# Row of the norm, first activations of down, and two first tiles: four pieces of work placed elsewhere in a one-core encoder block

## The chip, the core and the metric

The kernel runs on one core of a Trainium2 chip. A core has five engines with queues of their own: PE (TensorE, matmuls; its weight loads are listed apart as PEld), DVE (VectorE), ACT (ScalarE), POOL (GpSimd) and SP (SyncE, which here only issues transfers). The metric is the time on the device of one execution, in microseconds (us). Three runs of the kernel before gave 1122.03 to 1122.51 us, with a median of 1122.2 us.

## What is computed

One layer of an encoder block on 256 tokens of width 2048, in float32. Two mixers (a state-space scan in both directions and a pooling mixer) read one projection and share an output projection; a gated channel mixer follows, and then a gated embedding:

```python
h = h + rmsnorm(mix, mix_norm_post[i])
hn = rmsnorm(h, ffn_norm_pre[i])
up = hn @ w_up                                    # 2048 -> 2 x 5632
gate, val = jnp.split(up, 2, axis=-1)
gate = dwconv_centred(gate, conv_w, conv_b)       # 3 taps along the tokens
ff = (jax.nn.gelu(gate, approximate=True) * val) @ w_down   # 5632 -> 2048
h = h + rmsnorm(ff, ffn_norm_post[i])
gate = jax.nn.sigmoid(rmsnorm(h, ple_norm_pre[i]) @ w_ple_gate[i])
h = h + rmsnorm(gate * (p[i] @ w_ple[i]), ple_norm_post[i])
```

The change touches the part from "hn" to the gate's product. The stages are called wo (the output projection), up, down (dn), the embedding (ple) and the gate (gt).

## The kernel before

**Split numbers.** Each float32 operand is split into a high half (a cast on ACT, line 153) and a low half (source minus high half, a subtraction on DVE, line 154); a product is then three matmuls: high by high, high by low, low by high. The function is `split` (line 142). Raw weights arrive in a ring of three buffers of 1 MB (`raw`, line 157), the halves of 1024 columns go to rings of five (`whi`, `wlo`). A split whose name stands in `ready` was made earlier; one in `spare` has its own place. Larger tiles are pages, of which there are 13 (line 74).

**Who sets the order.** A planner orders the instructions of each engine by the order of the program and by its own estimate of when each is ready; a data dependency becomes a semaphore. `tc.issue_after(i)` puts what is traced inside behind instruction i on i's engine. Inside `with in_order():` (line 199) ACT, DVE and SP run exactly in the order of the program; PE is not bound by it.

**Up** (lines 966 to 980) is such an ordered block. It has 176 pieces, each of 512 rows by 256 columns of the weight, in order of slab (512 columns), gate or value, and half (256 columns); four pieces make a sum, in two accumulators. Five pieces are split ahead; at piece n, after its matmuls are traced, a finished sum is taken out (n % 4 == 3), piece n + 5 is split (`next_part`), then the convolution of the last gate's sum (`gate_conv`, at n % 4 == 0) and its gelu (n % 4 == 1) follow, and then the jobs kept for that piece (`jobs_at`): fetching, adding and storing the block sums of later weights (line 253), and sums of hidden activations. The gate's sums (`gate_out`, line 935) are multiplied by the row `rfb`, the reciprocal norm of each token laid along the tokens (line 941). The norm's factor comes out of `row_rstd` (line 398) as one number per partition; `along_tokens` (line 408) turns it: for each half of the tokens DVE copies the number to 128 columns (line 414), PE multiplies that with the identity, and DVE copies the result back (line 416). Up calls it ahead of its ordered block (line 876), and the first stage does so for its own row (line 535).

**Down** (`sublayer`, line 819, called on line 1036) has two halves of 1024 output columns, each of 22 units of two rows of tiles (`token_major`, line 305). Fifteen units of a half use seven products instead of eight (`seven_products`, line 255), for which sums of weight blocks, made in up and kept in DRAM, and sums of activations are loaded; the plain units are 0, 1, 6, 10, 17, 20 and 21. A plain unit has 24 matmuls of 512 columns, the others 21. The activations of a unit are split in `get_hid` (lines 989 and 990) into one of two buffers hs; all of these splits stand behind the last instructions of up's ordered block on ACT and DVE. `at` gives jobs to run ahead of a unit, in the second half only: ahead of unit 11 the first tile of the gate is loaded to a page and split to two more, and after the last unit the first tile of the embedding's second half is loaded and split in the rings, and the saved rows of h come back.

**The boundary.** After down's last sum come the norm, the new rows of h (line 848), their transposes (dnxt, line 391) and the split panel (dnx, lines 190 and 191), while PE has the embedding's matmuls to do; then the gate's.

Of the kernel before, what the change touches and what calls it, by code (L numbers as in the profile page):

```python
# [11 lines left out]
F32 = mybir.dt.float32  # L12
F32R = mybir.dt.float32r
AF = mybir.ActivationFunctionType
ALU = mybir.AluOpType
ORDERED = (mybir.EngineType.Activation, mybir.EngineType.DVE, mybir.EngineType.SP)

P = 128
L = 256
# [5 lines left out]
NF = DFF // P  # L25
# [28 lines left out]
def build(nc, a, out):  # L54
# [6 lines left out]
    with tile.TileContext(nc) as tc, \  # L61
# [15 lines left out]
        def mid(name, dtype=F32):  # L77
            return gp.tile([P, 1024], dtype, tag="mid", bufs=3, name=name)
# [10 lines left out]
        def mm(o, lhsT, rhs, start, stop):  # L89
            last["pe"] = ins(nc.tensor.matmul(o, lhsT, rhs, start=start, stop=stop, skip_group_check=True))  # L90
# [317 lines left out]
        def along_tokens(name, r):  # L408

            rb = sp.tile([P, L], F32, tag="rb", bufs=1, name=name)  # L410
            ps = misc(f"{name}p")
            for t in range(2):
                w = mid(f"{name}w{t}")
                nc.vector.tensor_copy(w[:, :P], r[t][:, 0:1].to_broadcast([P, P]))
                mm(ps[:, t * P:(t + 1) * P], w[:, :P], ident, True, True)
            nc.vector.tensor_copy(rb, ps[:, :L])
            return rb

# [397 lines left out]
                return dict(self.got[k], a11=(h1[:, :P], l1[:, :P]), a12=(h2[:, :P], l2[:, :P]),  # L816
                            a22=(h2[:, P:], l2[:, P:]))

        def sublayer(name, w, ks, get, gain, h, vnext, panel=Panel, fast=((), ()), sums=None, at=(), row=None):

            mg = [page(f"{name}m{t}") for t in range(2)]
            sq = [[], []]
            for half in range(2):
# [2 lines left out]
                acc = [main(f"{name}a{half}{t}") for t in range(2)]  # L826
                if fast[half]:
                    alt += main(f"{name}s{half}") if half else []
                token_major(f"{name}{half}", w, half * 1024, ks, get, acc, 1, fast[half], alt, sums, at if half else ())
                for t in range(2):  # L830
                    for n in range(2):
                        q = tiny(f"{name}q{t}{half}{n}", 1)
# [40 lines left out]

        pl = [ple(0)]
        rf = row_rstd("rf", h)
        rfb = along_tokens("rfb", rf)
        h_kept = []
        for t in range(2):
            h_kept.append(dp.tile([P, D], F32, tag=f"h{t}", bufs=1, name=f"h_kept{t}"))
# [18 lines left out]
        def hid_part(k):  # L898
            return hid[k // 8][:, (k % 8) * L:(k % 8 + 2) * L]

        def hid_sums_of(k, s, o):
            return pair_sums(f"he{k}", s, o, *(hid_part(k)[:, i * P:(i + 1) * P] for i in range(4)))

# [14 lines left out]
        for u in dn_stored:  # L918

            jobs_at[16 * (u // 2) + 4 * (u % 2) + 13].extend(hid_sums_jobs(2 * u))  # L920

        blocks = [(s, v, i) for s in range(DFF // 512) for v in range(2) for i in range(2)]
        parts, slab = [], {}
# [11 lines left out]
        def gate_out(s, i, acc):  # L935
            if i == 0:
                slab[s] = mid(f"gr{s}"), mid(f"fc{s}"), mid(f"ft{s}")
            o = slab[s][0][:, i * 512:(i + 1) * 512]
            total(o, acc)
            v = o.rearrange("p (f t) -> p f t", f=2)  # L940
            nc.vector.tensor_tensor(v, v, rfb.unsqueeze(1).to_broadcast([P, 2, L]), op=ALU.mult)

        def gate_conv(s, i):

# [21 lines left out]
        with in_order():  # L966
            for _ in range(5):
                next_part()
            for n in range(NPIECES):
                s, v, i = blocks[n // 4]  # L970
                if n % 4 == 0:
                    acc = main(f"{'gv'[v]}a{s}{i}")
                feature_pairs(n % 4, parts[n], hf, acc)
                if n % 4 == 3:
                    (value_out if v else gate_out)(s, i, acc)
                next_part()
                if n >= 4 and n % 4 < 2 and blocks[n // 4 - 1][1] == 0:
                    (gelu if n % 4 else gate_conv)(blocks[n // 4 - 1][0], blocks[n // 4 - 1][2])
                for job in jobs_at[n]:
                    job()  # L980
        ends = [chain[e] for e in ORDERED[:2]]

        cur = {}

        def get_hid(k):
            if k % 2 == 0:
                t = lp.tile([P, 1024], F32R, tag="hs", bufs=2, name=f"hs{k}")
                with tc.issue_after(ends[0]), tc.issue_after(ends[1]):
                    nc.scalar.copy(t[:, :512], hid_part(k))  # L989
                    nc.vector.tensor_sub(t[:, 512:], hid_part(k), t[:, :512].bitcast(F32))  # L990
                cur["t"] = t
            o = (k % 2) * L
            return cur["t"][:, o:o + L], cur["t"][:, 512 + o:512 + o + L]

# [17 lines left out]
                d = hid_sums_of(k, sp.tile([P, 512], F32, tag="junk", bufs=1, name=f"hs{k}"), o)  # L1012
            return dict(d, a11=(h1[:, :P], l1[:, :P]), a12=(h2[:, :P], l2[:, :P]), a22=(h2[:, P:], l2[:, P:]))

        def ple_parts():

            r = raw("ple1r0", w_ple[1, 0])
            for j in range(2):
                ready[f"ple10_{j}"] = split(f"ple10_{j}", r[:, j * 1024:(j + 1) * 1024], 1024)

        def back():

            for t in range(2):
                h[t] = page(f"hb{t}")
                last["dma"] = load(h[t], h_kept[t])

        def first():

            r, hi, lo = page("gtf"), page("gtfh", F32R), page("gtfl", F32R)
            last["dma"] = load(r, w_gate[0, 0])  # L1030
            for j in range(2):
                c = slice(j * 1024, (j + 1) * 1024)
                spare[f"gt00_{j}"] = hi[:, c], lo[:, c]
                ready[f"gt00_{j}"] = split(f"gt00_{j}", r[:, c], 1024)

        hp = sublayer("dn", w_down, list(range(NF)), hid_get, gload("gffn", a["ffn_norm_post"][0]), h, V_PN,
                      fast=dn_fast, sums=hid_sums, at={11: first, NF // 2: lambda: (ple_parts(), back())}, row=rf)


        pl = [page("plb")]  # L1040
# [154 lines left out]
```

## Time and profile before

| | |
|---|---|
| median of three runs | 1122.2 us |
| profiled execution | 1122.17 us |
| its span, first to last instruction | 1120.3 us |
| PE busy | 1107.4 us (99%), 5957 matmuls |
| DVE busy | 942.4 us (84%) |
| ACT busy | 716.7 us (64%) |
| POOL busy | 65.3 us (6%) |
| transfers | 336.54 MB, 300 GB/s in the mean |
| granted clock of PE | 0.999 |

A row of the timeline has the start in us from the span's start, the duration, the engine, the line of the program, the operation, output<-inputs (buffer numbers left out), the shape and the count; in brackets stands how long the engine had been idle before and what ended that. Matmuls overlap, so one that lasts 0.39 us is followed by the next after 0.23 us, and a busy PE is not yet a PE at its pace; gaps are read from starts. A list of waits has the engine, its instruction, what it waited for, the time in total, the count and the longest. Stages by that clock: wo until about 286 us, up from 293 to 788 us, down from 790 to 1014 us, the gate from 1020 us.

### The profile page before, as it was taken

What the parts mean: (1) busy time and instruction counts of PE and PEld (TensorE: products, weight loads), DVE (VectorE), ACT (ScalarE), POOL (GpSimd) and SP (SyncE); (2) the same over time, 40 slices, a digit from 0 to 9 for tenths busy, and PEclk for the clock granted to TensorE, in tenths of its full rate; (3) what the DMA queues carried; (4) which work ended last, traced back from release to release, by engine and by line L of the source; (5) the groups of instructions that cost most, each with busy time, mean ns of one, the idle gap of its engine ahead of it and who ended that gap; (6) DMA issues with size and microseconds to landing.
All of it is one profiled execution on the core that took longest, in us unless ns stands there. A gap on an engine that the chain in (4) does not pass through costs nothing.

```text
span 1120.3 us, 15956 instructions
## 1 busy us (share of the span) xinstructions
PE 1107.4 (99%) x5957; PEld 952.8 (85%) x5957; DVE 942.4 (84%) x1300; ACT 716.7 (64%) x1039; POOL 65.3 (6%) x133
## 2 busy tenths in 40 slices
PE   9999999999999999999999999999999999999997
PEld 9999988888888888888888888888788888877876
DVE  6569897899878888888878888888799899989795
ACT  6847663555775564655655656656688778867573
POOL 0200000100100000000000000000000000001001
PEclk9999999999999999999999999999999999999999
DMA  9752446454599999999889898989898799996663
GB/s 363 310 208 96 171 159 270 151 188 178 230 366 389 361 353 367 360 343 352 359 322 373 326 383 345 356 346 374 322 408 313 242 348 405 413 362 238 228 232 107
DMA packets 53070, 336.54 MB, mean 300 GB/s; under 512 B 5888, under 2 KB 6784, under 8 KB 19072
## 3 DMA queue, kind: packets, MB, share of 16 engines
q1 hardware_dynamic: 43200, 284.03, 65.6%
q0 software_dynamic: 9360, 50.86, 12.4%
q8 instruction: 47, 0.77, 0.3%
q10 hardware_dynamic: 432, 0.62, 0.2%
q14 instruction: 31, 0.25, 0.1%
HBM read 290.92 MB, written 44.56 MB: 299 GB/s over the span
## 4 chain that ended last, share of the span: by engine, by line
PE 94%; DVE 2%; ACT 2%; issue 1%; POOL 0%; DMA 0%; SPq 0%; POOLq 0%; ACTq 0%
PE va L90 22%; PE ga L90 21%; PE dna L90 12%; PE woa L90 7%; PE xbc L90 6%; PE gt L90 5%; PE z L90 4%; PE dtu L90 4%; PE dns L90 4%; PE dn0s L90 2%; PE dn1s L90 2%; PE pw L90 1%; PE yd L90 1%; PE ple L90 1%; DMA dtur<-w_dtu 0%
## 5 line engine op out<-in xcount | busy, mean ns | idle before, releaser
L90 PE MATMUL ga<-wox,ug_0h 128*128 128x512 f32 x352 | 125.6, 395 | 0.0
L90 PE MATMUL ga<-wox,ug_1h 128*128 128x512 f32 x352 | 125.1, 394 | 0.0
L90 PE MATMUL va<-wox,uv_0h 128*128 128x512 f32 x352 | 124.8, 393 | 0.0
L90 PE MATMUL va<-wox,uv_1h 128*128 128x512 f32 x352 | 124.7, 393 | 0.0
L90 PE MATMUL ga<-wox,ug_1l 128*128 128x256 f32 x352 | 99.1, 282 | 0.0
L90 PE MATMUL ga<-wox,ug_0l 128*128 128x256 f32 x352 | 99.1, 282 | 0.0
L90 PE MATMUL va<-wox,uv_0l 128*128 128x256 f32 x352 | 99.1, 281 | 0.0
L90 PE MATMUL va<-wox,uv_1l 128*128 128x256 f32 x352 | 98.9, 281 | 0.0
L253 DVE TENSOR_TENSOR dnb<-dnb 128x512 f32<-128x512 f32 x120 | 82.8, 690 | 3.1
L90 PEld LDWEIGHTS va<-wox,uv_0h 128*128 128x128 f32 x352 | 66.1, 188 | 15.0
L90 PEld LDWEIGHTS ga<-wox,ug_0h 128*128 128x128 f32 x352 | 66.1, 188 | 14.9
L90 PEld LDWEIGHTS ga<-wox,ug_1h 128*128 128x128 f32 x352 | 66.1, 188 | 14.9
L90 PEld LDWEIGHTS va<-wox,uv_1h 128*128 128x128 f32 x352 | 66.1, 188 | 14.9
L90 PEld LDWEIGHTS ga<-wox,ug_0l 128*128 128x128 f32 x352 | 66.2, 188 | 0.1
L90 PEld LDWEIGHTS va<-wox,uv_1l 128*128 128x128 f32 x352 | 66.2, 188 | 0.1
L90 PEld LDWEIGHTS ga<-wox,ug_1l 128*128 128x128 f32 x352 | 66.2, 188 | 0.0
L90 PEld LDWEIGHTS va<-wox,uv_0l 128*128 128x128 f32 x352 | 66.2, 188 | 0.0
L989 ACT CAST hs<-hid 128x512 fp32r<-128x512 f32 x44 | 27.2, 621 | 24.5 <-PE dna L90 24.3
L990 DVE TENSOR_TENSOR hs<-hid,hs 128x512 fp32r<-128x512 f32 x44 | 30.1, 686 | 10.2 <-ACT hs L989 10.2
L90 PE MATMUL dna<-dn_0h,hs 128*128 128x512 f32 x112 | 35.4, 394 | 1.8 <-issue 1.5
L90 PE MATMUL dna<-dn_1h,hs 128*128 128x512 f32 x112 | 35.6, 393 | 0.0
L244 POOL DMA_DIRECT2D dns<-dnb x28 | 15.2, 543 | 321.6 <-DVE dnb L253 297.3
(2128 smaller groups left out, 3159.6 us busy)
## 6 DMA issues: line engine op xcount, KB each, us to landing
dnb<-w_down SPq DMA_DIRECT2D x30, 1024.0 KB, 8.8
dns<-dnb POOLq DMA_DIRECT2D x28, 1024.0 KB, 5.1
hd<-hsum POOLq DMA_DIRECT2D x22, 512.0 KB, 7.8
zr<-w_z SPq DMA_DIRECT2D x8, 1024.0 KB, 4.9
dtur<-w_dtu SPq DMA_DIRECT2D x14, 528.0 KB, 8.6
wo0r<-w_out_ SPq DMA_DIRECT2D x7, 1024.0 KB, 4.8
dn0r<-w_down SPq DMA_DIRECT2D x7, 1024.0 KB, 7.0
dn1r<-w_down SPq DMA_DIRECT2D x7, 1024.0 KB, 8.0
```

What stands on the lines that cost most here:

```text
L90: last["pe"] = ins(nc.tensor.matmul(o, lhsT, rhs, start=start, stop=stop, skip_group_check=True))
L244: nc.gpsimd.dma_start(t, pg[0])
L253: nc.vector.tensor_add(v[:, i], v[:, i], v[:, j])
L989: nc.scalar.copy(t[:, :512], hid_part(k))
L990: nc.vector.tensor_sub(t[:, 512:], hid_part(k), t[:, :512].bitcast(F32))
```

## The change

Four things move.

- The row of the norm in up: `along_tokens` is called at piece 6 instead of ahead of the block, and its multiplication, convolution and gelu for the first sum follow there in one go; the other sums keep their places. Its two copies go to one buffer (junk) instead of two (mid), and its matmuls stand behind the last matmul traced before.
- The activations of down's first two units are split in up's order, at pieces 170 and 172, and no split of activations is tied to up's last instructions any more.
- The gate's first tile is loaded and split ahead of unit 17 of down's first half, instead of unit 11 of the second.
- The embedding's first tile is loaded and split ahead of unit 10 of the second half, instead of after it. Both come through the ring of raw buffers, and both have two pages for their halves.

```diff
@@ along_tokens
-            for t in range(2):
-                w = mid(f"{name}w{t}")
-                nc.vector.tensor_copy(w[:, :P], r[t][:, 0:1].to_broadcast([P, P]))
-                mm(ps[:, t * P:(t + 1) * P], w[:, :P], ident, True, True)
+            w = sp.tile([P, 512], F32, tag="junk", bufs=1, name=f"{name}w")
+            with tc.issue_after(last["pe"]):
+                for t in range(2):
+                    nc.vector.tensor_copy(w[:, t * P:(t + 1) * P], r[t][:, 0:1].to_broadcast([P, P]))
+                    mm(ps[:, t * P:(t + 1) * P], w[:, t * P:(t + 1) * P], ident, True, True)
@@ sublayer
-                token_major(f"{name}{half}", w, half * 1024, ks, get, acc, 1, fast[half], alt, sums, at if half else ())
+                token_major(f"{name}{half}", w, half * 1024, ks, get, acc, 1, fast[half], alt, sums, at[half])
@@ ahead of up
-        rfb = along_tokens("rfb", rf)
...
+        early_hs = {}
+
+        def hid_split(k):
+            t = lp.tile([P, 1024], F32R, tag="hs", bufs=2, name=f"hs{k}")
+            nc.scalar.copy(t[:, :512], hid_part(k))
+            nc.vector.tensor_sub(t[:, 512:], hid_part(k), t[:, :512].bitcast(F32))
+            return t
+
+        def first_hs(k):
+            early_hs[k] = hid_split(k)
...
+        for n, k in ((170, 0), (172, 2)):
+            jobs_at[n].append(lambda k=k: first_hs(k))
@@ gate_out
-            o = slab[s][0][:, i * 512:(i + 1) * 512]
-            total(o, acc)
-            v = o.rearrange("p (f t) -> p f t", f=2)
-            nc.vector.tensor_tensor(v, v, rfb.unsqueeze(1).to_broadcast([P, 2, L]), op=ALU.mult)
+            total(slab[s][0][:, i * 512:(i + 1) * 512], acc)
+            if s or i:
+                gate_norm(s, i)
+
+        def gate_norm(s, i):
+            if s == i == 0:
+                slab["rfb"] = along_tokens("rfb", rf)
+            v = slab[s][0][:, i * 512:(i + 1) * 512].rearrange("p (f t) -> p f t", f=2)
+            nc.vector.tensor_tensor(v, v, slab["rfb"].unsqueeze(1).to_broadcast([P, 2, L]), op=ALU.mult)
@@ up's loop
-                if n >= 4 and n % 4 < 2 and blocks[n // 4 - 1][1] == 0:
+                if n == 6:
+
+                    gate_norm(0, 0)
+                    gate_conv(0, 0)
+                    gelu(0, 0)
+                elif n >= 8 and n % 4 < 2 and blocks[n // 4 - 1][1] == 0:
                     (gelu if n % 4 else gate_conv)(blocks[n // 4 - 1][0], blocks[n // 4 - 1][2])
...
-        ends = [chain[e] for e in ORDERED[:2]]
@@ get_hid
-                t = lp.tile([P, 1024], F32R, tag="hs", bufs=2, name=f"hs{k}")
-                with tc.issue_after(ends[0]), tc.issue_after(ends[1]):
-                    nc.scalar.copy(t[:, :512], hid_part(k))
-                    nc.vector.tensor_sub(t[:, 512:], hid_part(k), t[:, :512].bitcast(F32))
-                cur["t"] = t
+                cur["t"] = early_hs.pop(k, None) or hid_split(k)
@@ the two tiles
-        def first():
-
-            r, hi, lo = page("gtf"), page("gtfh", F32R), page("gtfl", F32R)
-            last["dma"] = load(r, w_gate[0, 0])
+        def tile_ahead(name, src):
+
+            r, hi, lo = raw(f"{name}f", src), page(f"{name}fh", F32R), page(f"{name}fl", F32R)
             for j in range(2):
                 c = slice(j * 1024, (j + 1) * 1024)
-                spare[f"gt00_{j}"] = hi[:, c], lo[:, c]
-                ready[f"gt00_{j}"] = split(f"gt00_{j}", r[:, c], 1024)
+                spare[f"{name}_{j}"] = hi[:, c], lo[:, c]
+                ready[f"{name}_{j}"] = split(f"{name}_{j}", r[:, c], 1024)
+
+        def gate_ahead():
+            tile_ahead("gt00", w_gate[0, 0])
+
+        def ple_ahead():
+            tile_ahead("ple10", w_ple[1, 0])
@@ the call of down
-                      fast=dn_fast, sums=hid_sums, at={11: first, NF // 2: lambda: (ple_parts(), back())}, row=rf)
+                      fast=dn_fast, sums=hid_sums, at=({17: gate_ahead}, {10: ple_ahead, NF // 2: back}), row=rf)
```

More of the change, by code (lines that the diff above doesn't have):

```diff
@@ L817, in __call__, with sublayer @@
                             a22=(h2[:, P:], l2[:, P:]))
-        def sublayer(name, w, ks, get, gain, h, vnext, panel=Panel, fast=((), ()), sums=None, at=(), row=None):
+        def sublayer(name, w, ks, get, gain, h, vnext, panel=Panel, fast=((), ()), sums=None, at=((), ()), row=None):
             mg = [page(f"{name}m{t}") for t in range(2)]
@@ L1013, in hid_sums @@
             return dict(d, a11=(h1[:, :P], l1[:, :P]), a12=(h2[:, :P], l2[:, :P]), a22=(h2[:, P:], l2[:, P:]))
[L1015 to L1019, printed above, removed]
         def back():
```

## The prediction, as it was put on record

> **What bounds the kernel now.** I read the page's head first, then the list of waits of TensorE (PE), then the timelines of PE, VectorE (DVE) and ScalarE (ACT) around the four places that the diff touches.
>
> ```profile
> span 1120.3 us, 15956 instructions
> ...
> PE 1107.4 (99%) x5957; PEld 952.8 (85%) x5957; DVE 942.4 (84%) x1300; ACT 716.7 (64%) x1039; POOL 65.3 (6%) x133
> ```
>
> PE is busy for 1107.4 of 1120.3 us, so the 12.9 us in which it stands are nearly all that moved work can win. DVE (84%) has room as a mean, but a mean over stages; each stage has to be asked by itself. The profiled execution took 1122.17 us: 1.87 us lie outside its span, and it is 0.03 us under the median of 1122.2, so a sum made against the span carries over to the median.
>
> ```profile
> PE gt L90 <- DVE gt_0l L154: 0.9, 1, 0.9
> ...
> PE rfbp L90 <- DVE rfbw L414: 0.5, 1, 0.5
> ```
>
> These two waits, and a third of 1.47 us which is shown below, are what the change goes for: rfbp is the matmul that turns the norm's row, gt_0l the low half of a tile of the gate. Together they are 2.9 us.
>
> **The change part by part.** The parts are A (the row, in up), B (down's first activations), C (the boundary from down to the gate) and D (the two tiles split in mid-down).
>
> **A, the row.** The wait of 0.5 us at rfbp goes, since the row's inputs are long there at piece 6. But the moved work lands in an order that is written out: ACT and DVE run up's instructions exactly as the program gives them. Before, piece 3's sum and the row come first, then piece 9's split, gate_conv, piece 10's split, gelu. Afterwards the row's two copies, the copy back, the multiplication, gate_conv and gelu stand in one block behind piece 11's split, and behind that block wait piece 7's sum and the split of piece 12. Each step of the block needs the one before it on the other engine, so the queue stands while the chain runs to and fro. What it starts from:
>
> ```profile
> L120 SPq DMA_DIRECT2D uv00r<-w_up x2: 862/917/972, 305.8 to 306.7; - x2
> ...
> DMA to landing us min/median/max: 9.0/9.7/10.5
> ```
>
> The two loads for pieces 8 to 11 are issued at 305.8 and 306.7 and land after 9.0 and 10.5 us, so pieces 10 and 11 have their data at 317.2, whatever happens to the row; the pieces were late because of the load and not because of the row. Next, the durations, from DVE and ACT of before:
>
> ```profile
> 309.96 0.23 DVE L414 COPY rfbw<-rf1r 128x128 f32<-128x128 f32 x1 [1.64 <-POOL rf1r L381]
> 310.77 0.43 DVE L416 COPY rfb<-rfbp 128x256 f32<-128x256 f32 x1 [0.58 <-PE rfbp L90]
> ...
> 321.82 2.87 DVE L253 TENSOR_TENSOR dnb<-dnb 128x512 f32<-128x512 f32 x4
> 324.61 1.22 DVE L154 TENSOR_TENSOR uv_1l<-uv00r,uv_1h 128x1024 fp32r<-128x1024 f32 x1
> 325.74 0.74 DVE L371 TENSOR_TENSOR gr<-gr,ga 128x256 f32<-128x256 f32 x2
> 326.52 0.69 DVE L941 TENSOR_TENSOR gr<-gr,rfb 128x512 f32<-128x512 f32 x1
> 327.13 1.22 DVE L154 TENSOR_TENSOR uv_0l<-uv01r,uv_0h 128x1024 fp32r<-128x1024 f32 x1
> ...
> 329.72 0.69 DVE L951 TENSOR_TENSOR fc<-fc,ft 128x510 f32<-128x510 f32 x1 [0.23 <-ACT ft L949]
> 330.51 0.69 DVE L952 TENSOR_TENSOR fc<-fc,gr 128x510 f32<-128x510 f32 x1
> ```
>
> ```profile
> 319.62 1.03 ACT L153 CAST uv_0h<-uv00r 128x1024 fp32r<-128x1024 f32 x1
> 320.67 1.28 ACT L956 ACT_TABLE_LOAD   x1
> ...
> 323.44 0.64 ACT L370 COPY gr<-ga 128x256 f32<-128x256 f32 x2
> 323.96 1.06 ACT L153 CAST uv_0h<-uv01r 128x1024 fp32r<-128x1024 f32 x1
> ...
> 327.25 0.60 ACT L948 ACTIVATE fc<-gr,vt 128x256 f32<-128x256 f32 x1 [1.28 <-DVE gr L941]
> ...
> 330.14 1.04 ACT L153 CAST uv_0h<-uv01r 128x1024 fp32r<-128x1024 f32 x1
> ```
>
> In steps: ACT casts piece 10 from 317.2 to 318.3 (1.03), DVE subtracts until 319.6 (1.2 with its start). The block sums of piece 5 take 2.79 from start to next start: 322.4. Piece 11's subtraction, 1.13 to the next start: 323.5. The row's two copies at 0.23: 323.9. The matmul and its wait 0.58, the copy back 0.43: 324.9. The multiplication 0.61: 325.5. gate_conv on ACT lasts 2.89 (327.25 to 330.14) and lets DVE add after 2.47: 328.0; the second add ends 1.48 later: 329.5. ACT is free at 328.4, and the load of gelu's table (1.28) follows directly on a cast in the row above, so it ends at 329.7 and hides most of that; gelu takes about 0.55 until piece 7's copies start (an estimate from the multiplication's 0.61): 330.3. The cast of piece 12 follows 0.52 later and ends at 331.9. DVE adds after the first copy (0.78), multiplies (0.61), and subtracts piece 12 (1.22): 333.3. Now what PE asks for:
>
> ```profile
> 319.32 0.39 PE L90 MATMUL va<-wox,uv_0h 128*128 128x512 f32 x1
> ```
> ```profile
> 319.48 22.31 PE va L90 x128
> ```
>
> Piece 8 starts at 319.32, and 128 matmuls of eight pieces take 22.31, 2.79 a piece: piece 12 starts at 330.49 and reads its low half at 330.7. In before that half is ready at 328.35, 2.4 us early. Afterwards it is there at 333.3, so PE stands for 2.6 us. Behind it the block sums of piece 10 come before piece 16: 333.3 and piece 13 (1.13), then gate_conv, bound by ACT, to piece 14 at 337.9, piece 15 at 339.6, block sums 342.4, a sum and product 1.4, piece 16 at 344.9, asked for at 330.7 + 2.6 + 11.16 = 344.5: another 0.4. Later pieces have more cover. The 0.5 us that was won at rfbp isn't to be taken off again, because these ends are counted from the load. I take **+3.0**. The ends: -0.5 if the block is covered after all, for which DVE would have to come to it some 3 us earlier; and +4.7 if the planner, which orders PE by its own estimate, takes the load to be quick and puts the row's matmuls at the start of piece 8 (319.3), where they wait for the copies until 324.05.
>
> One rule speaks against the part. The Trainium skill ("ScalarE: Activation LUTs", What ACT_TABLE_LOAD costs) says that a switch of tables costs 1283 ns and a drain of some 1380 ns. The trace has the 1.28 us and no drain: 0.02 us lie between the cast's end and the load. With the drain on the chain the sum would be 1.4 us more, by the page.
>
> along_tokens also serves the row of the first stage (rxb). Its copies go to another buffer and its matmuls behind the last one traced, where they stand anyway; I cost it at nothing, with a wait like rfbp's (0.5) as its price if I am wrong.
>
> **B, down's first activations.**
>
> ```profile
> 788.23 0.28 PE L90 MATMUL va<-wox,uv_1l 128*128 128x256 f32 x1
> 789.98 0.70 PE L90 MATMUL dna<-dn_0h,hs 128*128 128x512 f32 x2 [1.47 <-issue]
> ```
> ```profile
> 789.73 0.41 DVE L371 TENSOR_TENSOR hid<-hid,va 128x256 f32<-128x256 f32 x1
> ```
> ```profile
> 785.00:788.00 3.00, 3.00 (x20) 2.63 (x19) 1.41 (x2) 1.05 (x1) 0.00 (x0) 1.00 0.84 348
> ```
>
> The last matmul of up starts at 788.23 and is followed 0.12 later in the stream's own pace, but down starts at 789.98, since its activations are split behind up's last sum. Split at pieces 170 and 172 they are long ready: 1.63 us are free. What is late next is the accumulators: PE has six such buffers, and the last two of up are read until 789.73 + 0.41 = 790.14. The first six matmuls (0.23 each) run until 789.74, so up to 0.5 may stay, or nothing where the planner takes the other weights first. I take **-1.4**, between -1.1 and -1.6. The four added instructions lie in up's last pieces, where DVE has room (the last row: 1.41 of 3 us busy); if that cover went, they would cost DVE 2 x 0.69, by the rows of its halves of 128x512. The gain is kept through down because DVE's work moves up with PE: two subtractions fewer are left for it there.
>
> **C, the boundary.**
>
> ```profile
> 1024.30 0.63 PE L90 MATMUL gt<-gt_0h,dnxh 128*128 128x512 f32 x2
> 1025.78 0.73 PE L90 MATMUL gt<-gt_0l,dnxh 128*128 128x512 f32 x2 [0.85 <-DVE gt_0l L154]
> ```
> ```profile
> 1011.23 1.22 DVE L154 TENSOR_TENSOR ple_0l<-ple1r,ple_0h 128x1024 fp32r<-128x1024 f32 x1
> 1012.36 1.22 DVE L154 TENSOR_TENSOR ple_1l<-ple1r,ple_1h 128x1024 fp32r<-128x1024 f32 x1
> ...
> 1017.51 0.75 DVE L848 SCALAR_TENSOR_TENSOR hb<-dnm,dn1r,hb 128x512 f32<-128x512 f32 x1 [0.44 <-POOL dn1r L381]
> ```
>
> PE could go on at 1024.76 and does at 1025.78, 1.0 us later, plus about 0.1 behind it. DVE has split the embedding's tile from 1011.23 to 1013.5; without that, the next tile of the gate takes its place (its raw buffer comes free one load earlier too), and gt_0l is ready some 10 us before its use. The panel's own chain isn't quicker: hb waits at 1017.51 for POOL's dn1r. I take **-1.1**; the ends are 0 (if the planner spends the room otherwise, or the embedding's matmuls, which cover the wait for dn1r, are drawn ahead) and -1.3.
>
> **D, the splits in mid-down.** The gate's tile moves from unit 11 of the second half to ahead of unit 17 of the first; the embedding's goes ahead of unit 10. In before the gate's split cost nothing, as it came behind the splits of unit 10, a plain one that lasts long on PE:
>
> ```profile
> 950.94 2.35 DVE L154 TENSOR_TENSOR gtfl<-gtf,gtfh 128x1024 fp32r<-128x1024 f32 x2
> ```
>
> Ahead of unit 17 it comes in front of what PE wants next:
>
> ```profile
> 871.85 1.22 DVE L154 TENSOR_TENSOR dn_0l<-dn0r,dn_0h 128x1024 fp32r<-128x1024 f32 x1
> ...
> 874.12 0.69 DVE L990 TENSOR_TENSOR hs<-hid,hs 128x512 fp32r<-128x512 f32 x1
> ```
> ```profile
> 875.20 0.62 PE L90 MATMUL dna<-dn_0h,hs 128*128 128x512 f32 x2
> 875.66 0.62 PE L90 MATMUL dna<-dn_0l,hs 128*128 128x512 f32 x2
> 876.12 1.09 PE L90 MATMUL dna<-dn_0h,hs 128*128 128x512 f32 x4
> ```
>
> DVE is without a gap there. The two subtractions (2.27 from start to next start) push unit 17's to 875.3 and 876.4 and the low half of the activations (874.12 + 0.69) to 877.1; PE wants it at 876.12. So PE stands about **+1.1**, once, and then DVE catches up, since a plain unit asks less of it than it lasts. The ends: 0, if the planner puts the tile behind unit 17's own splits, and +2.3, if all of it shows. At unit 10 the same order meets more lead, and the gate's split is gone from unit 11: 0. Of the transfers, the two loads of 1 MB now go through the ring of three raw buffers on SP's queue, so that each of the next loads is issued one slot later:
>
> ```profile
> 868.98 0.33 SPq L120 DMA_DIRECT2D dn038r<-w_down  x1
> ```
> ```profile
> dn0r<-w_down SPq DMA_DIRECT2D x7, 1024.0 KB, 7.0
> ```
>
> Unit 18's load then goes out at 868.98 and lands by 876.0 (7.0); PE comes to unit 18 after 24 matmuls of 0.23, at 880.7, so 4 us of cover are left. The saved rows come back (hb) from the same place as before. Two pages more are held at the end of the second half, which the freed pages of the hidden layer make up for.
>
> **The sum**: 3.0 - 1.4 - 1.1 + 1.1 = +1.6 us, from 1122.2 to **1123.8**. A difference of 0.2%, 2.2 us, is about what a measurement of this kernel can tell from no change: below 1120.0 is faster, above 1124.4 slower. The forecast lies inside, on the slow side.
>
> **The rivals.**
>
> *The row's block is covered* (A is -0.5). For it: PE has four pieces in hand, 11 us. Against it: DVE's rows above, whose block sums come first. Then -0.5 - 1.4 - 1.1 + 1.1 = -1.9, 1120.3; and where the change doesn't do what D says (the planner leaves unit 17's splits first), -3.0, 1119.2. Chance 0.30.
>
> *The row's matmuls are placed too early and PE waits in them* (the slower side). Place: the start of piece 8 in up; price 4.7 in place of 3.0, so +3.3, 1125.5. It decides as soon as the planner's place for them lies more than 3 us ahead of the copies' end. For it: the wait at rfbp in before is one such misjudgement; against it: that one was only 0.5. Chance 0.12.
>
> *The table's load isn't hidden* but starts when gelu's inputs are there (329.5 instead of 328.4): +1.1, 1124.9. Against it: the load started 0.02 after a cast. Chance 0.05. The drain of the Trainium skill's page, named above, would act in this way.
>
> *DVE is the bound in down*, and all 2.3 of D shows: +2.8, 1125.0. For it: no gap on DVE at unit 17; against it: it has to wait for PE soon after. Chance 0.07.
>
> **How the numbers follow.** The forecast has 0.46, with a range of its own from 1122.7 to 1125.2 (A from 2.5 to 3.8, B and C by 0.3 each either way); 0.29 of it lies within 0.2% and 0.17 above. The covered row gives 0.22 faster and 0.08 the same. The three slow cases are slower: 0.24. Faster 0.22, same 0.37, slower 0.41. The range from 1119.6 to 1126.0 leaves out a tenth on either side.
>
> **What would show it.** A: a wait of PE at piece 12 (va <- uv_0l) of 2 to 3 us near 331, with ACT's cast of that piece some 7 us later than now; its absence disproves the step, and a wait at rfbp of over 3 us shows the second rival. B: the gap ahead of the first dna matmul shrinks from 1.47 to at most 0.5. C: no wait on gt_0l. D: the gate's subtractions ahead of unit 17's on DVE, and PE's wait on hs behind them. The prediction is wrong if up isn't longer than now.

## The result and the profile after

Six executions of the changed kernel took 1127.26 to 1130.78 us, with a median of 1128.45; six of the kernel before, on the same chip, had a median of 1122.34. The ratio is 1.0056, with a 95% interval of 1.0043 to 1.0069: 6.1 us slower. The profiled execution took 1130.78 us, the longest of the six, so its rows show the loss at its largest (8.5 us of span).

Head of the page of the kernel after:

```profile
span 1128.8 us, 15956 instructions
...
PE 1112.6 (99%) x5957; PEld 955.7 (85%) x5957; DVE 942.2 (83%) x1300; ACT 715.0 (63%) x1039; POOL 67.0 (6%) x133
```

Its list of waits of PE:

```profile
PE va L90 <- ACT uv_0h L153: 4.2, 1, 4.2
...
PE va L90 <- DVE uv_0l L154: 0.5, 1, 0.5
```

The wait at rfbp and the one on gt_0l are gone, as they should be, and a wait of 4.2 us stands in up, where none was. It is not the whole loss. The table follows six kernels through the program: the start of PE's first matmul at some place, less the start of the same matmul before (profiled executions, us).

| PE's first matmul of | after | row alone | hs alone | tiles alone | gate's tile alone | all but the row |
|---|---|---|---|---|---|---|
| piece 8 of up | -1.08 | -1.17 | +0.66 | +0.05 | +0.12 | +0.52 |
| unit 2, half 0 of down | +5.67 | +7.40 | -1.07 | +0.03 | +0.11 | -1.21 |
| unit 19, half 0 | +5.66 | +7.40 | -1.07 | +0.02 | +1.22 | -1.22 |
| unit 2, half 1 | +6.59 | +7.41 | -1.06 | +0.90 | +3.15 | -0.45 |
| unit 11, half 1 | +6.59 | +7.40 | -1.07 | +0.89 | +3.14 | -0.45 |
| unit 18, half 1 | +9.08 | +7.41 | -1.06 | +1.44 | +2.26 | +0.56 |
| unit 4, half 0 of the gate | +8.58 | +7.41 | -1.09 | +0.95 | +0.61 | +0.05 |

What stands at piece 8 in the kernels that leave the row alone (up to +0.66) comes from the stages ahead, where nothing was changed; it differs from one execution to the next. The column of after jumps in four places: up (+6.75, of which B is -1.73, by the column of hs alone, where the activations alone are moved), the end of half 0 (+0.9), units 12 to 14 of half 1 (+2.5) and the boundary (-0.5).

**Up.** DVE, then ACT, then PE of the kernel after, around the row:

```profile
323.82 0.22 DVE L415 COPY rfbw<-rf1r 128x128 f32<-128x128 f32 x1
326.54 0.42 DVE L417 COPY rfb<-rfbp 128x256 f32<-128x256 f32 x1 [2.50 <-PE rfbp L90]
```

```profile
327.72 0.60 ACT L966 ACTIVATE fc<-gr,vt 128x256 f32<-128x256 f32 x1 [8.18 <-DVE gr L959]
...
330.72 1.28 ACT L974 ACT_TABLE_LOAD   x1
...
333.07 1.06 ACT L153 CAST uv_0h<-uv01r 128x1024 fp32r<-128x1024 f32 x1
```

```profile
329.74 0.28 PE L90 MATMUL va<-wox,uv_1l 128*128 128x256 f32 x1
334.18 0.89 PE L90 MATMUL va<-wox,uv_0h 128*128 128x512 f32 x2 [4.16 <-ACT uv_0h L153]
335.61 0.80 PE L90 MATMUL va<-wox,uv_0l 128*128 128x256 f32 x2 [0.54 <-DVE uv_0l L154]
```

The row's copies end at 324.04, where the forecast had 323.9. The copy back then stands 2.50 us for the four matmuls: they are in PE's order, but 2 us behind the copies. ACT's convolution, which has stood 8.18 us, starts at 327.72 instead of the forecast's 325.5, and everything behind it is late by those 2.2 us; the table's load follows the convolution at once. PE's row at 329.74 is the last of piece 11, and the next begins at 334.18. What lies around that is in the windows (length, PE's busy time, its granted clock, share of the DMA engines, GB/s):

```profile
331.17:334.58 3.41, 0.40 (x2) 1.00 0.41 173
334.58:341.41 6.83, 6.29 (x21) 0.50 0.42 154
341.41:344.82 3.41, 3.41 (x21) 1.00 0.54 171
```

```profile
337.48 0.63 PE L90 MATMUL va<-wox,uv_0h 128*128 128x512 f32 x1
338.12 0.63 PE L90 MATMUL va<-wox,uv_0h 128*128 128x512 f32 x1
```

The clock is 0.50 for 6.83 us, from 334.58 to 341.41, and a pair of matmuls takes 0.64 us (337.48 to 338.12) instead of the 0.35 of up's own pace.

**Down.** SP's queue in half 1, before and after, and ACT's and PE's rows behind it:

```profile
933.32 0.33 SPq L120 DMA_DIRECT2D dn1r<-w_down  x1
```

```profile
939.91 0.33 SPq L120 DMA_DIRECT2D ple10f<-w_ple_  x1
...
947.67 0.33 SPq L120 DMA_DIRECT2D dn1r<-w_down  x1
```

```profile
959.50 0.62 ACT L153 CAST dn122ah<-dn122r 128x512 fp32r<-128x512 f32 x1 [1.30 <-DMA dn122r<-w_down]
```

```profile
982.89 0.50 PE L90 MATMUL dna<-dn128dl,hs 128*128 128x512 f32 x1 [0.53 <-DVE dn128dl L154]
```

The embedding's tile (ple10f) takes a slot of the ring, and down's next load, that of unit 10, goes out at 947.67 instead of 933.32: 6.6 of the 14.35 us is the general delay, 7.8 is the slot. From unit 11 on ACT waits for loads, four times until unit 13 and for 2.3 us in all (in the kernel before once, 1.14 us), and in units 12 to 14 PE waits for the splits.

### The profile page after: what moved, and what is told of

It reads as the page before. It is cut to its first block, busy times and chain, and to the rows that moved or that the text cites. A ratio compares the mean times of both kernels' runs of the same rounds, so it can differ in the third digit from the quotient of the medians.

```text
span 1128.8 us, 15956 instructions
## 1 busy us (share of the span) xinstructions
PE 1112.6 (99%) x5957; PEld 955.7 (85%) x5957; DVE 942.2 (83%) x1300; ACT 715.0 (63%) x1039; POOL 67.0 (6%) x133
## 4 chain that ended last, share of the span: by engine, by line
PE 89%; DVE 5%; ACT 2%; issue 2%; DMA 2%; POOL 0%; POOLq 0%; SPq 0%; ACTq 0%; DVEq 0%
PE ga L90 22%; PE va L90 22%; PE dna L90 9%; PE woa L90 7%; PE xbc L90 6%; PE gt L90 5%; PE dtu L90 4%; PE z L90 4%; PE dns L90 2%; PE dn1s L90 1%; PE dn0s L90 1%; DMA dn122t<-dns 1%; DMA dn036r<-w_down 1%; PE pw L90 1%; PE yd L90 1%
```

## The experiments

All ran five rounds beside the kernel before, whose median was 1122.3 to 1122.5 in each; differences are against that.

**One part at a time.** Four kernels, cut along the diff: the change without the row's move; the row's move alone; down's first activations alone; the two tiles alone.

```diff
 # row_back: the change, with along_tokens("rfb", rf) ahead of up again
 # row_only: before, with
-        rfb = along_tokens("rfb", rf)
...
+                if n == 6:
+                    gate_norm(0, 0); gate_conv(0, 0); gelu(0, 0)
 # hs_only: before, with
+        for n, k in ((170, 0), (172, 2)):
+            jobs_at[n].append(lambda k=k: first_hs(k))
 # tiles_only: before, with
+                      at=({17: gate_ahead}, {10: ple_ahead, NF // 2: back})
```

> The changed kernel with the norm's row put back ahead of up (the other three moves stay). Theory 1, read from the two traces: the row's block is what cost up its 7.4 us in the profiled execution (some 5 us in the median, since that execution was the slowest of six), so this kernel comes to 1123.0 to 1124.0 us: the kernel before, less 1.6 for down's first activations, plus 0.9 at the end of down's half 0, plus 2.5 in its half 1, less 0.5 at the boundary. Rival, as the forecast had it: the row costs 3.0 and the two tiles nothing, then this kernel is at 1125.4 or above only if the rest of the loss is in down whatever the row does.

> The kernel before with the row's move alone. Theory 1: TensorE stands over 4 us ahead of piece 12 and then runs at a low granted clock for some 7 us; the time is 4 to 7.5 us above the kernel before, 1126.5 to 1130 us, and the spread over the executions is wider than that of the kernel before, since the clock's fall need not come each time. Rival (the forecast): 3.0 us above, 1125.3, with the clock at 1.0.

> The kernel before with down's first activations split inside up's order, nothing else. Theory 1 and the forecast agree: 1.4 to 1.7 us below the kernel before, 1120.6 to 1120.9 us. Rival: the gap only moves to the first weights of down, and the time is that of the kernel before within 0.3 us.

> The kernel before with the two tiles' moves alone. Theory 1: the end of half 0 costs 0.9, units 12 to 15 of half 1 cost 2.5, the boundary to the gate gives 0.5: 2.9 us above the kernel before, 1125.2 us. Rival 1 (the forecast): unit 17 costs 1.1, the boundary gives 1.1, half 1 nothing: 1122.3 us. Rival 2: half 1's loss comes of the changed turn of the activations' buffers, not of the tiles: then this kernel is within 0.5 us of the kernel before.

| kernel | median | difference | ratio, 95% interval |
|---|---|---|---|
| row_back | 1122.33 | -0.1 | 1.0000 (0.9992 to 1.0009) |
| row_only | 1129.34 | +6.9 | 1.0061 (1.0048 to 1.0074) |
| hs_only | 1120.99 | -1.4 | 0.9986 (0.9977 to 0.9995) |
| tiles_only | 1124.10 | +1.7 | 1.0014 (1.0005 to 1.0023) |

The row's move is the loss. The parts add up to +7.2, and the change has +6.1; the intervals of the parts are wider than the difference. My expectation for the row held, and that for the activations to 0.1; the tiles cost less than the trace of after had made me expect (1.7, not 2.9), and so the kernel without the row came out 0.7 us lower than the range that I gave. That trace is the longest execution of its six, and tiles_only alone spreads from 1122.67 to 1125.19 where the kernel before spreads by 0.9.

**What the row's 6.9 us are made of.** Four kernels from row_only: matmuls of no use in the place where PE stood (row_fill); the row's own matmuls moved up in PE's order (row_tight); both (row_tight_fill); and the row's work spread over four pieces (row_spread).

```diff
 # row_fill, and row_tight_fill with 24
+                if n == 12:
+                    for i in range(40):
+                        nc.tensor.transpose(ps[:, :P], ident, ident)
 # row_tight: pieces' matmuls of n == 10 from the second quarter on stand behind rfbp's
+                    with tc.issue_after(behind) if behind and kk else nullcontext():
 # row_spread
-                if n == 6:
-                    gate_norm(0, 0); gate_conv(0, 0); gelu(0, 0)
+                if n == 5: slab["rfb"] = along_tokens("rfb", rf)
+                if n == 6: gate_norm(0, 0)
+                if n == 7: gate_conv(0, 0)
+                if n == 8: gelu(0, 0)
```

> The kernel before with the row's move alone, and 40 matmuls of 128x128 with no use between pieces 11 and 12 on TensorE, where it stood 4.2 us (about 0.09 us each, 3.6 us, all inside the stand); they write a PSUM bank that nobody reads. The block on ScalarE and VectorE is unchanged. Theory 1 (the stand lowers the granted clock afterwards): the clock stays at 1.0 in the 8 us behind the stand, a pair of matmuls of piece 12 takes 0.35 instead of 0.64 us, and the time falls by 2.5 to 3.5 us against the row's move alone, to 1126.0 to 1126.8 us, with the stand itself unchanged. Rival (the clock falls for another reason, such as the transfers or the other engines): the time stays at 1129.3 or rises by up to 0.5 us.

> The row's move alone, with TensorE's order mended: the row's four matmuls stand behind the first quarter of piece 10, not in its middle, so that VectorE's copy out of PSUM no longer stands 2.5 us. Theory 1 (of the move's 6.9 us some 2 are those matmuls' late place, some 2 the clock's fall after a stand over 4 us, the rest the block that the forecast priced): the stand at piece 12 falls from 4.2 to 2.4 to 2.9 us, the clock stays at 1.0, and the time is 1125.0 to 1126.0 us. Rival 1: the clock falls after a stand of 2.5 us as well: 1127 to 1127.6 us. Rival 2: the place of the matmuls is not what held the block: 1129 us.

> The row's move alone with its matmuls placed behind the first quarter of piece 10, and 24 matmuls of 128x128 with no use (2.6 us) between pieces 11 and 12, inside the stand of 2.8 us; they write a PSUM bank that nobody reads. Theory 1 (what is left is the block that the forecast priced): the clock stays at 1.0 behind the stand, and the time is 1125.5 to 1126.3 us, 3.0 to 3.8 above the kernel before, of which the forecast had 3.0. Rival: the clock still falls, 1127.5 to 1128.5 us.

> The kernel before with the row's move, but its work in up spread over pieces 5 to 8 (row at 5, product with it at 6, convolution at 7, gelu at 8) instead of all at piece 6, so that no cast of a weight tile waits behind the whole chain. Theory 1 (the cost is the in-order block, not the row's place): no stand above 1 us, the clock at 1.0, and the move's gain ahead of up (1.1 to 1.3 us) shows, less 0.4 for the row's four matmuls: 1121.2 to 1122.0 us. Rival (the work itself is too much for ScalarE and VectorE in pieces 6 to 14, wherever it stands): TensorE still stands 2 us or more near 331, 1124 us or above.

| kernel | median | difference | ratio, 95% interval |
|---|---|---|---|
| row_only | 1129.34 | +6.9 | 1.0061 (1.0048 to 1.0074) |
| row_fill | 1127.31 | +4.8 | 1.0043 (1.0029 to 1.0057) |
| row_tight | 1128.00 | +5.5 | 1.0049 (1.0035 to 1.0063) |
| row_tight_fill | 1125.90 | +3.6 | 1.0032 (1.0020 to 1.0044) |
| row_spread | 1125.70 | +3.2 | 1.0028 (1.0017 to 1.0038) |

A window of row_only, the same of row_fill, and PE's rows of row_fill:

```profile
334.00:338.00 4.00, 3.22 (x10) 0.59 0.12 20
```

```profile
334.00:338.00 4.00, 3.29 (x20) 1.00 0.13 16
```

```profile
329.71 4.53 PE L983 MATMUL fill<-ident 128*128 128x128 f32 x40
334.03 0.72 PE L90 MATMUL va<-wox,uv_0h 128*128 128x512 f32 x2
```

The block on ACT and DVE is the same, piece 12 starts at 334.03 instead of 334.09, and yet the clock stays at 1.0 and 2.1 us are won (2.5 to 3.5 were expected). (The 0.59 is the mean of a window with 0.50 in most of it.) So the fall of the clock belongs to PE's standing, and it has a price of its own. In row_tight the matmuls stand at 324.58 (rows of PE, then windows):

```profile
324.58 0.61 PE L90 MATMUL rfbp<-ident,rfbw 128*128 128x128 f32 x4
332.86 0.73 PE L90 MATMUL va<-wox,uv_0h 128*128 128x512 f32 x2 [2.77 <-ACT uv_0h L153]
334.29 0.80 PE L90 MATMUL va<-wox,uv_0l 128*128 128x256 f32 x2 [0.70 <-DVE uv_0l L154]
```

```profile
330.50:333.91 3.41, 0.73 (x2) 1.00 0.66 279
333.91:337.32 3.41, 3.03 (x10) 0.50 0.21 41
```

The stand falls to 2.77 us, as expected, but the clock falls all the same: rival 1, though the time is 0.4 us above its range. This execution was the shortest of five (1127.14), and the low clock is over at 337.32 in it, after 3.41 us. With the stand filled as well (row_tight_fill) the clock is 1.0:

```profile
329.88 2.78 PE L985 MATMUL fill<-ident 128*128 128x128 f32 x24
332.82 0.73 PE L90 MATMUL va<-wox,uv_0h 128*128 128x512 f32 x2 [0.15 <-ACT uv_0h L153]
```

```profile
334.00:338.00 4.00, 3.75 (x22) 1.00 0.35 100
```

The expectation held. The steps, each from neighbours in the table: late matmuls 1.4 (6.9 - 5.5; these two intervals overlap, but in the traces piece 12 starts 1.23 us earlier, 332.86 against 334.09), the clock 2.0 to 2.1 (6.91 - 4.83, 5.54 - 3.56; the intervals overlap here too, but every execution with the stand filled is shorter than every one of its neighbour without), and 3.6 for the block itself.

row_spread missed its expectation by 4 us. Its DVE and ACT:

```profile
322.71 0.42 DVE L417 COPY rfb<-rfbp 128x256 f32<-128x256 f32 x1 [2.58 <-PE rfbp L90]
323.05 2.86 DVE L253 TENSOR_TENSOR dnb<-dnb 128x512 f32<-128x512 f32 x4
...
326.96 0.68 DVE L944 TENSOR_TENSOR gr<-gr,rfb 128x512 f32<-128x512 f32 x1
```

```profile
327.68 0.61 ACT L952 ACTIVATE fc<-gr,vt 128x256 f32<-128x256 f32 x1 [6.62 <-DVE gr L944]
```

The row's copies come four us earlier (319.78, against 323.64), but the matmuls stand 2 us behind them again, and then the block sums of 2.86 us lie in front of the product. The convolution starts at 327.68, as in row_only (327.63). What the spreading gains is only that the casts no longer wait for all of the chain: PE stands 1.64 us and the clock doesn't fall. Its time lies where the rival (too much work there) had it, above 1124, but PE's stand is shorter than the rival's 2 us and the row's matmuls are late again, so the rival is not shown, and neither is my theory that the block's form alone costs; the chain's start is set by the same two things, the matmuls' place and the block sums.

**The tiles.** The gate's tile alone; both tiles loaded into pages and not into the ring; only the embedding's tile into a page.

```diff
 # gate_only: the embedding's tile stays after the last unit of half 1
-    {10: ple_ahead, NF // 2: back}
+    {NF // 2: lambda: (ple_parts(), back())}
 # tiles_page (both tiles) and ple_page (the embedding's)
-            r, hi, lo = raw(f"{name}f", src), ...
+            r, hi, lo = page(f"{name}f"), ...
```

> The kernel before with the gate tile's move alone (unit 17 of half 0, ring buffer); the embedding's tile stays at unit 16 of half 1, as before. Theory 2: half 0's end still costs 0.9, half 1 loses its 0.5 to 2.5 and the boundary keeps its gain, so 1122.6 to 1122.9 us. Rival (the loss in half 1 comes of the gate's page being gone over, its two kept tiles holding two pages longer): still 1124 us.

> The kernel before with the two tiles' moves alone, but each tile is loaded into a page instead of a buffer of the weights' ring of three. Theory 2 (the ring's turn delays down's own loads): the 0.9 at half 0's end and the 0.5 to 2.5 in half 1 go, the boundary's 0.5 stays: 1121.9 us. Rival (VectorE has no slack for the tiles' splits, 2.4 us each): unchanged, 1123.5 to 1124.5 us. A second rival: the pages are as scarce as the ring, and the time rises.

> The two tiles' moves alone, with the gate's tile loaded into the weights' ring as in the change and only the embedding's tile loaded into a page of its own. Theory 2 (the ring's slot is what costs half 1 and part of the boundary): no wait of ScalarE for down's loads in units 11 to 15 of half 1, and the time of the gate's move alone, 1121.0 to 1121.6 us. Rival 1 (the tile's splits and its two kept pages cost it): 1123 to 1124 us, as with the tile in the ring. Rival 2: the page that it takes costs what the slot did.

| kernel | median | difference | ratio, 95% interval |
|---|---|---|---|
| tiles_only | 1124.10 | +1.7 | 1.0014 (1.0005 to 1.0023) |
| tiles_page | 1122.84 | +0.4 | 1.0004 (0.9995 to 1.0013) |
| ple_page | 1122.78 | +0.4 | 1.0006 (0.9998 to 1.0015) |
| gate_only | 1121.04 | -1.4 | 0.9986 (0.9977 to 0.9995) |

None of the three expectations was met. The gate's tile gains 1.4 us by itself, where 0.1 to 0.4 of loss was expected (the column of the first table, with +3.15 in half 1, is the longest of its eleven executions); the embedding's loses 3.1 (1124.10 against 1121.04). The two kernels with pages lie between theory 2 and its rival. SP's queue with its load in a page (ple_page):

```profile
933.29 0.42 SPq L120 DMA_DIRECT2D ple10f<-w_ple_  x1
934.78 0.33 SPq L120 DMA_DIRECT2D dn1r<-w_down  x1
```

Down's load goes out at 934.78, 1.46 later than before, which is just that execution's delay, and ACT waits for no load between units 11 and 15. So the slot is real, at some 1.3 us of the median (1.7 less 0.4; the two intervals overlap, so the size is less sure than the mechanism, which the rows show). Nearly 2 us remain with the embedding's tile. By the traces they lie in two places: 0.9 at unit 17 of half 1 and 1.1 at the boundary. At unit 17 the kernel before loses 0.9, waiting for a split:

```profile
987.03 1.18 PE L90 MATMUL dna<-dn_0h,hs 128*128 128x512 f32 x4 [0.28 <-ACT dn_0h L153]
```

In gate_only this wait is gone (PE is 3.14 behind at unit 16 and 2.26 at unit 18); in ple_page and tiles_only, where the embedding's tile is split from unit 10 on, it is there as before. The expectation's "unit 16" for the place where that tile stays in gate_only is a slip: it is split after the last unit. DVE at the boundary, in gate_only and then in ple_page:

```profile
1011.22 1.22 DVE L154 TENSOR_TENSOR ple_0l<-ple1r,ple_0h 128x1024 fp32r<-128x1024 f32 x1
...
1014.08 1.40 DVE L838 SCALAR_TENSOR_TENSOR dnm<-dna,rf0r,gffn 128x512 f32<-128x512 f32 x2
...
1016.36 0.74 DVE L848 SCALAR_TENSOR_TENSOR hb<-dnm,dn0r,hb 128x512 f32<-128x512 f32 x1
```

```profile
1014.71 1.56 DVE L838 SCALAR_TENSOR_TENSOR dnm<-dna,rf0r,gffn 128x512 f32<-128x512 f32 x2 [1.96 <-ACT dnj L837]
1016.46 1.23 DVE L154 TENSOR_TENSOR gt_0l<-gt0r,gt_0h 128x1024 fp32r<-128x1024 f32 x1 [0.18 <-ACT gt_0h L153]
...
1018.26 1.22 DVE L154 TENSOR_TENSOR gt_1l<-gt0r,gt_1h 128x1024 fp32r<-128x1024 f32 x1
...
1020.05 0.74 DVE L848 SCALAR_TENSOR_TENSOR hb<-dnm,dn0r,hb 128x512 f32<-128x512 f32 x1
```

Where the embedding's tile was split before (1011.22 and behind it), DVE has nothing else to do until the sums of squares are there: in ple_page it stands 1.96 us at that place. The planner then puts the two splits of the gate's next ring tile (gt_0l, gt_1l, 1.2 us each) between the norm's products, and the first new row of h starts at 1020.05 instead of 1016.36. The kernel after has the same order:

```profile
1024.09 1.23 DVE L154 TENSOR_TENSOR gt_0l<-gt0r,gt_0h 128x1024 fp32r<-128x1024 f32 x1 [0.18 <-ACT gt_0h L153]
...
1027.69 0.74 DVE L849 SCALAR_TENSOR_TENSOR hb<-dnm,dn0r,hb 128x512 f32<-128x512 f32 x1
```

In the profiled executions PE gains 1.6 between unit 18 and the gate in gate_only and only 0.5 with the embedding's tile moved. No kernel was run that holds the gate's splits back there, so that the order is the cause of the 1.1 is read from the rows, not tried; nor was the wait at unit 17.

**Putting together what pays.** The activations and the gate's tile; the same with the gate's tile ahead of unit 10; the same (unit 17) with the row at piece 2 of up, with its users left where they were before.

```diff
 # hs_gate = before + hs_only + gate_only;  hs_gate10
-    {17: gate_ahead}
+    {10: gate_ahead}
 # hs_gate_row2 = hs_gate, with
-        rfb = along_tokens("rfb", rf)
...
+                if n == 2:
+                    rfb_.append(along_tokens("rfb", rf))
```

> The kernel before with down's first activations split inside up's order and the gate's tile at unit 17 of half 0; the row and the embedding's tile stay where they were. Theory 2 (parts add up): 1.4 for each, 1119.6 us (1119.0 to 1120.4). Rival: the activations' buffers, turned by the early split, take the gate's gain: 1121 us.

> As the kernel with the activations and the gate's tile, but the gate's tile is split ahead of unit 10 of half 0 instead of unit 17. Theory 3 (what is left of the loss at half 0's end is VectorE's lead, 2.4 us of splits too close to the half's end, and it has ten units to win it back here): 0.5 to 1.5 us below the version with unit 17, 1118.3 to 1119.2 us. Rival (the loss comes from two pages held, or from the ring of three, wherever the tile stands): the same as unit 17 or above it, since the pages are held longer.

> As the kernel with the activations and the gate's tile, and the norm's row inside up's order at piece 2, so ahead of its first use instead of behind it; the product, the convolution and the gelu stay where they were before. Theory 1 (the row ahead of up costs TensorE 1.3 us, and the move's loss comes only of dragging its users along): 0.7 to 1.1 us below the kernel without this, 1118.6 us. Rival: VectorE's in-order copy waits for the row's matmuls there too and holds the next split: 1 us or more above.

| kernel | median | difference | ratio, 95% interval |
|---|---|---|---|
| hs_gate | 1119.04 | -3.4 | 0.9969 (0.9958 to 0.9981) |
| hs_gate10 | 1119.78 | -2.7 | 0.9975 (0.9966 to 0.9985) |
| hs_gate_row2 | 1118.28 | -4.2 | 0.9963 (0.9951 to 0.9976) |

All three beat both kernels, the first as expected: the parts add up. At unit 10 the loss at the end of half 0 is gone, as theory 3 had it (1.75 us in hs_gate's profiled execution, none here), but between there and the gate PE wins back 0.9 and not 2.5, so the time is no lower and the expectation of 1118.3 to 1119.2 was missed. At the boundary PE has two waits that hs_gate's trace doesn't have, 0.37 for gt_0l and 0.36 for dnxl; why the planner's order there is another isn't settled. The row inside up seems to pay if it stays ahead of its first use: DVE's rows of hs_gate_row2,

```profile
312.25 0.42 DVE L417 COPY rfb<-rfbp 128x256 f32<-128x256 f32 x1 [0.81 <-PE rfbp L90]
...
313.37 0.69 DVE L954 TENSOR_TENSOR gr<-gr,rfb 128x512 f32<-128x512 f32 x1
```

with a wait of 0.81 that nobody needs. PE reaches piece 8 at 318.46 (0.86 before the kernel before), 1.1 earlier than in hs_gate; between the medians it is 0.8, with intervals that overlap.

## Why the prediction was wrong

It forecast +1.6 and the change has +6.1, above the range. The sign was right, and so was the place of the largest term; the sizes, point by point:

- **A, the row: +3.0 forecast, +6.9 measured.** The chain was followed to 0.2 us as far as the row's copies. The step that failed is "The matmul and its wait 0.58": that row came from a place where PE was already waiting for the copies (0.5 at rfbp), and here the planner put the matmuls 2 us behind them (1.4 of the median). The forecast had looked at the opposite mistake (matmuls too early, PE waiting in them) and had given that a rival; the late side had none. And the sum priced PE's stand at its length, with the pace behind it unchanged. The clock's fall (2.0) was missing, and with it a price that no row of up in before shows, since PE never stands that long there; in that trace the clock falls only at the very end (last section). With both taken away, 3.6 is left (2.2 to 4.9 by the interval) against 3.0: the block was sized rightly.
- **B: -1.4 forecast, -1.4 measured.** The gap is gone: the first matmul of down follows the last of up by 0.12, in up's own pace:

```profile
795.63 0.28 PE L90 MATMUL va<-wox,uv_1l 128*128 128x256 f32 x1
795.75 0.62 PE L90 MATMUL dna<-dn_0h,hs 128*128 128x512 f32 x2
```

- **D at unit 17: +1.1 forecast.** PE doesn't stand there, because the planner laid the tile's two splits between those of unit 16. The lead that DVE lost shows in units 19 to 21, at the half's end, where PE loses 0.9 in after:

```profile
903.58 0.51 PE L90 MATMUL dna<-dn_0h,hs 128*128 128x512 f32 x1 [0.31 <-DVE hs L906]
```

  The place was wrong, and the step that DVE would then catch up in a plain unit. The size was about right in after; with the gate's tile and no embedding's tile PE loses more there, 1.75 in hs_gate and 3.0 in gate_only's longest execution. That it is DVE's lead agrees with hs_gate10, where it doesn't come.
- **D at unit 10 of half 1: 0 forecast, and this was a missed term.** "At unit 10 the same order meets more lead" weighed DVE, and the ring's slot was weighed at unit 18 alone ("4 us of cover are left"). Unit 10's load is one slot, 7.8 us, later, ACT stands for loads from unit 11 on, and PE loses 2.5 us in the profiled execution, some 1.3 in the median.
- **C: -1.1 forecast.** With the gate's tile alone a gain comes (1.6 at the boundary in the trace of gate_only, -1.4 in all), but not by the forecast's mechanism: the embedding's tile is still split at 1011.22 there, and PE has no wait on gt_0l all the same. With the embedding's tile moved as well, gt_0l is early, as the forecast had it, and yet only 0.5 is left: the forecast had named the end (0, "if the planner spends the room otherwise, or the embedding's matmuls [...] are drawn ahead") and chosen against it. DVE's split of that tile had been lying in a hole; taking it out gained nothing, and by the rows the hole's place was given to work that delays the panel.

Of the rivals, none came to pass in after: the row's block is not covered, PE doesn't wait in the row's matmuls, the table's load follows its predecessor at once, and 0.9 of D's 2.3 shows. C and D together were forecast at 0 and measured at +1.7.

## What to carry to other kernels

When work is moved later into a written-out order, its users move with it: ask how far they are from their own first need, and move the producer only as far as leaves them in place (the row at piece 2 gained some 0.8, at piece 6 with its users it lost 6.9). Two stands of TensorE, of 4.2 and 2.8 us, cost some 2 us more than their length here, because the matmuls behind them ran at half the clock for 3.4 to 6.8 us; a chain that crosses to another engine needs that engine's order too, not only its duration. Before moving a load into a shared ring, ask which later load takes one slot more, at every place and not only the first; and ask whether the work taken away lay in a hole.

## What the runs showed of the hardware

The granted clock falls to 0.50 behind a stand of PE of 4.2 us, for 6.83 us (after, 334.58 to 341.41; row_only, 334.69 to 341.52), and also behind one of 2.77 us, for 3.41 us (row_tight, 333.91 to 337.32). It doesn't fall behind two stands of 1.64 and 0.53 us (row_spread), nor when matmuls of no use fill the stand.

The falls and rises keep to steps of 3.41 us: in after those at 334.58, 341.41 and 1123.06 are 2 and 229 steps apart. The step ahead of each fall in up is nearly empty: PE is busy for 0.40 us of it in after, 0.60 in row_only and 0.73 in row_tight. In row_spread the stands fall into two steps, counted back from the fall at 1118.00 at its end:

```profile
332.94:336.35 3.41, 2.82 (x16) 1.00 1.01 425
336.35:339.76 3.41, 1.83 (x9) 1.00 0.55 233
```

In the kernel before the clock falls only at the end of the span, where PE has little left to do:

```profile
1114.06:1117.47 3.41, 1.12 (x2) 1.00 0.66 217
1117.47:1120.31 2.84, 0.00 (x0) 0.50 0.34 109
```

So in these traces a fall follows a step that PE leaves mostly empty, and where a stand lies among the steps matters beside its length: row_spread's 1.64 us are shared by two. The share that is enough they don't give: at the ends of the spans a step with 1.52 us busy is followed by a fall in after (1119.65 to 1123.06) and by none in row_tight (1115.56 to 1118.97).

The Trainium skill ("TensorE: Matmul & The Clock Gate", Part 1: The HAM clock gate) says that the array's clock drops to half after an idle window of about 3.4 us and comes back after a busy window of the same length, with windows that run freely. The traces agree with it in the half clock and in the length of the step, and with its free run in that the steps don't begin with the stand. None of the windows ahead of the falls was idle throughout, though, and the stand of 2.77 us is shorter than such a window and had the fall nevertheless: 2.36 us of it lie in the window and 0.32 of the wait of 0.70 that follows close behind. The last fall of before follows a window with 2.29 us empty, so the stand alone may have been enough; no run separates the two. The low clock in after lasted for two such windows, in row_tight for one. The forecast could have drawn on this rule: a stand of 2.6 us lies near its bound, and would have been a rival.

The load of gelu's table is 1.28 us and follows the instruction ahead of it by 0.02 us in the chain of after, too (330.70 to 330.72), and gelu follows it by 0.01.
